# Weight tiles with 512 spare bytes, and blocks at changing offsets in them, in a float32 decoder layer

## The chip, the cores and the metric

The kernel runs on one core of one Trainium2 chip. The metric is device time in microseconds (us), from the start of the program to its end on that core.

## The reference

One layer of a hybrid decoder on 512 positions with 1024 channels, all in float32: half a gated FFN, a mixer, half a second gated FFN, a final norm.

```python
for l in range(DEPTH):                       # DEPTH = 1
    x = x + 0.5 * swiglu_ffn(rmsnorm(x, norm_ffn1[l]), ffn1_w_in[l], ffn1_w_out[l])
    x = x + hybrid_mixer(rmsnorm(x, norm_mix[l]), ...)
    x = x + 0.5 * swiglu_ffn(rmsnorm(x, norm_ffn2[l]), ffn2_w_in[l], ffn2_w_out[l])
return rmsnorm(x, norm_final)
```

`swiglu_ffn` is `(silu(x @ w_g) * (x @ w_u)) @ w_out` with 2816 hidden channels. The mixer projects to eleven parts of 1024 channels: a gated linear recurrence with 8 heads (HGRN2), a gated linear recurrence per channel (RG-LRU), a 31-tap causal convolution, and three gates. Each of the three branches is projected, gated and summed, and the sum goes through an output projection.

## The kernel before

**Numbers and products.** Each float32 operand is split into a high part (rounded to float32r, a form that TensorE multiplies faster) and a low part (the rest). A product is three matmuls: high weights with high activations (L255), high weights with low activations (L256), low weights with high activations (L257). A weight block is 128x128, the activations that stream past it are 128x512 (channels by positions).

**Weights.** All weights lie in DRAM in the order of use, in chunks of 16 blocks. `fetch` loads a chunk into one of two `raw` tiles. `_split_unit` (L214 to L239) turns half a chunk, a **unit** of 8 blocks, into a high tile `whi` (ScalarE, L230) and a low tile `wlo` (VectorE, L233). There are four buffers of each, and a unit is split two units before it is used. So a unit feeds 24 long matmuls. Units 0 to 43 are the first FFN's input weights, 44 to 65 its output weights, 66 to 185 the mixer's, 186 to 229 the second FFN's input weights, 230 to 251 its output weights. In all but the last stage the weights are the stationary operand, which TensorE loads ahead of a matmul. In the last stage (`last`, L533 to L535) four blocks side by side are a row of 512 columns that streams, and the activations are stationary.

**Pages.** Everything else of 128x512 lives in `NPAGES` pages of 2048 bytes per partition. `page` takes the oldest entry of the queue `free_pages`, `drop` puts a page at its end. A page's next owner waits until the last reader of the former one is done.

**Order.** The program is written in order of dependence, and a scheduler arranges the instructions of each engine by priorities that the kernel sets (`high_priority`, the filler taps of the convolution between other work, `issue_after`). On the chip each engine runs its list strictly in order.

**The mixer's parts that the prediction names.** `hgrn` (one call per head) makes `q` (L692) and `k`, then seven levels, each with small float32 matmuls on `q` and `k` (L749) and updates on VectorE; `dgs` and the state `st` end in the head's output (L776 with `dgs` as stationary operand, L778 with `q[:, t, :]`). `q` is a view of a tile with 132 columns per 128 positions:

```python
qx = self.tiny.tile([P, NTOK, P + 4], F32, tag="qx", name=self.name("q"), bufs=2)
q = qx[:, :, :P]
```

The 31-tap convolution is 30 VectorE operations per 128 channels (L607) that read and write `s` columns apart:

```python
s = CONVK - 1 - k
nc.vector.scalar_tensor_tensor(out=cv[1][:, s:], in0=cu[1][:, :S - s], scalar=w(k),
                               in1=cv[1][:, s:], op0=ALU.mult, op1=ALU.add)
```

`z` is the output of the second recurrence, eight pages, split at L297/L298 ahead of the projection of branch 1. `gw` are that recurrence's gate weights, four pages that are loaded and split (L297/L298) while the first FFN ends; they are first used at L632.

Of the kernel before, what the change touches and what calls it, by code (L numbers as in the profile page):

```python
# [12 lines left out]
F32R = mybir.dt.float32r  # L13
# [4 lines left out]
P = 128  # L18
# [112 lines left out]
    return m  # L131


class Kernel:
    NPAGES = 73
    CHUNK = 16
    UNIT = 8
    RBUFS = 2
# [10 lines left out]
    def __init__(self, ctx, tc, d):  # L149
# [5 lines left out]
        self.ps = ctx.enter_context(tc.tile_pool(name="ps", bufs=4, space=bass.MemoryType.PSUM))  # L155
        self.free_pages = deque(range(self.NPAGES))
        self.uid = 0
# [56 lines left out]
    def _split_unit(self):  # L214
        nc = self.nc
        u = self.next_unit
        if u * self.UNIT >= self.n_blocks:
            return
        per = self.CHUNK // self.UNIT
        c = u // per  # L220
        while self.next_raw <= c:
            self.fetch()
        o = (u % per) * self.UNIT
        raw = self.raws[c][:, o:o + self.UNIT, :]
        hi = self.ring.tile([P, self.UNIT, P], F32R, tag="whi", name=f"whi{u}", bufs=self.WBUFS)
        lo = self.ring.tile([P, self.UNIT, P], F32R, tag="wlo", name=f"wlo{u}", bufs=self.WBUFS)
        step = self.UNIT // 2 if u < 2 else self.UNIT
        for a in range(0, self.UNIT, step):
            z = slice(a, a + step)
            i = nc.scalar.activation(out=hi[:, z, :], in_=raw[:, z, :], func=AF.Copy)  # L230
            if u == self.MARK:
                self.mark = i
            self.last_lo = nc.vector.tensor_tensor(out=lo[:, z, :], in0=raw[:, z, :], in1=hi[:, z, :].bitcast(F32),  # L233
                                                   op=ALU.subtract)
        self.units[u] = (hi, lo)
        self.next_unit += 1
        if u % per == per - 1:
            del self.raws[c]
            self.fetch()  # L239
# [778 lines left out]
```

## Time and profile before

| | |
|---|---|
| Time, median of 3 runs | 1503.06 us (1501.24 to 1503.09) |
| Profiled execution: time | 1501.5 us |
| Profiled execution: span from first to last instruction | 1499.5 us |
| TensorE busy | 1486.5 us (99%), 6960 matmuls |
| VectorE busy | 897.3 us (60%) |
| ScalarE busy | 562.9 us (38%) |
| DMA, mean over the span | 93 GB/s, 139.55 MB |
| Granted TensorE clock, mean | 0.998 of full speed |

A row of the timeline has the start in us from the span's first instruction, the length in us, engine, line, operation and tiles as out<-in, with xN for N that follow each other, and in brackets the idle time before it with what ended it. Matmuls overlap: their starts tell the pace, and their lengths are longer than the step from one to the next. In a windows row, (xN) counts the instructions that reach into the window.

### The profile page before, as it was taken

Reading aid. Unit: us, or ns where it says so; the run is one execution under the profiler, and the core shown is the slowest. Engines: PE = TensorE matmul, PEld = TensorE weight load, DVE = VectorE, ACT = ScalarE, POOL = GpSimd, SP = SyncE. Lnnn points to the kernel's source line nnn. Section 1 sums busy time; section 2 is a strip of 40 time slices with the busy share of each in tenths; the row PEclk is TensorE's granted clock in tenths of the full one; section 3 lists DMA queues with packets and bytes.
Section 4 is the critical chain, followed back from the end, with each engine's and each line's share of the span. In section 5 each row is a group of like instructions: output and inputs, shape, how many; then the busy total and the mean of one; then the engine's idle time right before and its main releaser. Section 6 shows DMA issues by size and latency. Waiting matters only on the chain.

```text
span 1499.5 us, 17155 instructions
## 1 busy us (share of the span) xinstructions
PE 1486.5 (99%) x6960; PEld 1233.7 (82%) x6960; DVE 897.3 (60%) x1334; ACT 562.9 (38%) x822; POOL 21.8 (1%) x33
## 2 busy tenths in 40 slices
PE   9999999999999999999999999999999999999998
PEld 7888888888888888788887878888888888888887
DVE  7644444434877788898788995662554444444232
ACT  6322222223434345744456413453343222222122
POOL 0000000000000000000000000000000000000000
PEclk9999999999999999999999999999999999999999
DMA  6232322224222121212121222222232232322221
GB/s 239 85 113 85 102 95 90 107 85 141 84 90 108 57 85 60 82 61 81 57 85 56 85 97 101 84 98 99 87 110 85 84 112 85 101 97 102 109 85 56
DMA packets 22830, 139.55 MB, mean 93 GB/s; under 512 B 2656, under 2 KB 2912, under 8 KB 6880
## 3 DMA queue, kind: packets, MB, share of 16 engines
q1 hardware_dynamic: 22032, 137.41, 26.4%
q8 instruction: 55, 0.90, 0.2%
q10 hardware_dynamic: 720, 1.05, 0.2%
q14 instruction: 23, 0.19, 0.0%
HBM read 136.35 MB, written 2.10 MB: 92 GB/s over the span
## 4 chain that ended last, share of the span: by engine, by line
PE 66%; DVE 7%; ACT 2%; issue 1%; POOL 0%; POOLq 0%; ACTq 0%
PE acc L256 17%; PE acc L255 17%; PE acc L257 17%; DVE cv L607 3%; PE aux L749 3%; PE acc L534 2%; PE acc L535 2%; PE acc L533 2%; DVE wlo L233 1%; PE aux L533 1%; PE aux L534 1%; PE aux L535 1%; DVE th L670 1%; PE aux L739 0%; DVE gt L669 0%
## 5 line engine op out<-in xcount | busy, mean ns | idle before, releaser
L255 PE MATMUL acc<-hi,whi 128*128 128x512 f32 x1808 | 709.7, 393 | 0.2 <-ACT hi L305 0.2
L256 PE MATMUL acc<-lo,whi 128*128 128x512 f32 x1808 | 706.7, 391 | 1.0 <-DVE lo L298 1.0
L257 PE MATMUL acc<-hi,wlo 128*128 128x512 f32 x1808 | 706.9, 391 | 0.3 <-DVE wlo L233 0.3
L230 ACT ACTIVATE whi<-raw 128x1024 fp32r<-128x1024 f32 (+1 forms) x254 | 267.0, 1053 | 783.1 <-PE acc L256 526.1
L233 DVE TENSOR_TENSOR wlo<-raw,whi 128x1024 fp32r<-128x1024 f32 (+1 forms) x254 | 308.1, 1215 | 249.5 <-ACT whi L230 249.1
L257 PEld LDWEIGHTS acc<-hi,wlo 128*128 128x128 f32 x1808 | 339.8, 188 | 71.1 <-DVE wlo L233 0.7
L256 PEld LDWEIGHTS acc<-lo,whi 128*128 128x128 f32 x1808 | 340.0, 188 | 70.9 <-DVE lo L298 1.4
L255 PEld LDWEIGHTS acc<-hi,whi 128*128 128x128 f32 x1808 | 340.0, 188 | 70.2 <-issue 1.2
L607 DVE SCALAR_TENSOR_TENSOR cv<-cu,small,cv 128x507 f32<-128x507 f32 (+16 forms) x240 | 173.4, 732 | 3.3
L473 DVE TENSOR_TENSOR g<-g,acc 128x512 f32<-128x512 f32 x43 | 29.5, 687 | 107.6 <-PE acc L257 107.6
L470 DVE TENSOR_TENSOR g<-acc,bc 128x512 f32<-128x512 f32 x43 | 29.7, 691 | 101.8 <-PE acc L257 101.7
L749 PEld LDWEIGHTS aux<-q,k 128*127 128x127 f32 (+5 forms) x384 | 45.7, 183 | 11.1 <-DVE q L692 3.5
L749 PE MATMUL aux<-q,k 128*127 128x64 f32 (+5 forms) x384 | 46.5, 263 | 3.5 <-DVE q L692 3.0
L534 PE MATMUL acc<-wlo,hi 128*128 128x512 f32 (+1 forms) x132 | 46.7, 354 | 0.0
L535 PE MATMUL acc<-whi,lo 128*128 128x512 f32 (+1 forms) x132 | 46.7, 354 | 0.0
L533 PE MATMUL acc<-whi,hi 128*128 128x512 f32 (+1 forms) x132 | 46.6, 353 | 0.0
L752 DVE COPY_PREDICATED dgs<-masks,aux 127x256 f32<-127x256 uint8 (+4 forms) x40 | 26.5, 663 | 10.6 <-PE aux L749 10.3
L472 DVE TENSOR_TENSOR g<-g,sg 128x512 f32<-128x512 f32 x44 | 30.1, 686 | 0.7 <-ACT sg L471 0.7
L298 DVE TENSOR_TENSOR lo<-g,hi 128x512 fp32r<-128x512 f32 x44 | 30.0, 684 | 0.7 <-ACT hi L297 0.7
L297 ACT ACTIVATE hi<-g 128x512 fp32r<-128x512 f32 x44 | 27.0, 615 | 3.3 <-DVE g L473 3.3
L533 PEld LDWEIGHTS acc<-whi,hi 128*128 128x128 f32 x132 | 24.9, 189 | 4.1
L534 PEld LDWEIGHTS acc<-wlo,hi 128*128 128x128 f32 x132 | 24.9, 189 | 4.0
(204 smaller groups left out, 1010.0 us busy)
## 6 DMA issues: line engine op xcount, KB each, us to landing
raw<-w SPq DMA_DIRECT2D x124, 1024.0 KB, 4.8
x<-x SPq DMA_DIRECT2D x8, 256.0 KB, 6.0
raw<-w SPq DMA_DIRECT2D x8, 256.0 KB, 6.1
gw<-gw SPq DMA_DIRECT2D x4, 256.0 KB, 3.6
y<-xt SPq DMA_DIRECT2D x4, 256.0 KB, 2.1
y<-xt ACTq DMA_DIRECT2D x4, 256.0 KB, 2.5
gain<-nfin SPq DMA_DIRECT2D x2, 256.0 KB, 4.1
mk<-masks SPq DMA_DIRECT2D x1, 256.0 KB, 4.9
```

The costliest lines, as they stand in the source:

```text
L230: i = nc.scalar.activation(out=hi[:, z, :], in_=raw[:, z, :], func=AF.Copy)
L233: self.last_lo = nc.vector.tensor_tensor(out=lo[:, z, :], in0=raw[:, z, :], in1=hi[:, z, :].bitcast(F32), op=ALU.subtract)
L255: nc.tensor.matmul(out, lhsT=hi, rhs=xh[1], start=(k == 0), stop=False)
L256: nc.tensor.matmul(out, lhsT=hi, rhs=xl[1], start=False, stop=False)
L257: self.last_mm = nc.tensor.matmul(out, lhsT=lo, rhs=xh[1], start=False, stop=(k == n - 1))
L298: nc.vector.tensor_tensor(out=lo[1], in0=src, in1=hi[1].bitcast(F32), op=ALU.subtract)
L472: tt(out=g[1], in0=g[1], in1=sg[1], op=ALU.mult)
L533: nc.tensor.matmul(ps, lhsT=a, rhs=hi, start=(k == 0), stop=False)
L534: nc.tensor.matmul(ps, lhsT=a, rhs=lo, start=False, stop=False)
L535: nc.tensor.matmul(ps, lhsT=b, rhs=hi, start=False, stop=(k == FT - 1))
L607: nc.vector.scalar_tensor_tensor(out=cv[1][:, s:], in0=cu[1][:, :S - s], scalar=w(k), in1=cv[1][:, s:], op0=ALU.mult, op1=ALU.add)
L749: nc.tensor.matmul(pl[:w, t * 64:(t + 1) * 64].rearrange("p (b m) -> p b m", m=m), lhsT=k[1][:, t * P:t * P + w], rhs=ends(q[:, t, :], m), ...
```

## The change

Each `whi` and `wlo` tile is 128 float32 elements (512 bytes) longer. The 8 blocks of a unit lie together, but they begin at an element that `weight_offset` gives for the unit, for the high and the low tile apart. In the first FFN's input the offset starts at zero and grows by 64 bytes every five units, in its output only the low tile has one, in the second FFN's input it goes through 16, 32, 48, 96, 160, 224, 288, 352, 416, 480 and 8 bytes for four units each, in the second FFN's output by 64 bytes every three units. The mixer's units have none. The eight longer tiles take 4096 bytes per partition more; there is one page less.

```diff
--- before.py
+++ after.py
@@ -131,8 +131,24 @@
     return m
 
 
+def weight_offset(u):
+    if 4 <= u < 44:
+        a = 16 * ((u - 4) // 5)
+        return a, a
+    if 44 <= u < 65:
+        return 0, 16 * ((u - 44) // 3 + 1)
+    if 186 <= u < 230:
+        a = (4, 8, 12, 24, 40, 56, 72, 88, 104, 120, 2)[(u - 186) // 4]
+        return a, a
+    if 230 <= u < 251:
+        a = 16 * ((u - 230) // 3 + 1)
+        return a, a
+    return 0, 0
+
+
 class Kernel:
-    NPAGES = 73
+    NPAGES = 72
+    SLACK = 128
     CHUNK = 16
     UNIT = 8
     RBUFS = 2
@@ -222,8 +238,10 @@
             self.fetch()
         o = (u % per) * self.UNIT
         raw = self.raws[c][:, o:o + self.UNIT, :]
-        hi = self.ring.tile([P, self.UNIT, P], F32R, tag="whi", name=f"whi{u}", bufs=self.WBUFS)
-        lo = self.ring.tile([P, self.UNIT, P], F32R, tag="wlo", name=f"wlo{u}", bufs=self.WBUFS)
+        n = self.UNIT * P
+        wt = lambda what: self.ring.tile([P, n + self.SLACK], F32R, tag=what, name=f"{what}{u}", bufs=self.WBUFS)
+        hi, lo = [t[:, a:a + n].rearrange("p (b n) -> p b n", n=P)
+                  for t, a in zip((wt("whi"), wt("wlo")), weight_offset(u))]
         step = self.UNIT // 2 if u < 2 else self.UNIT
         for a in range(0, self.UNIT, step):
             z = slice(a, a + step)
```

The offsets alone leave every engine's list as it was. With one page less the queue of free pages turns sooner, and the scheduler arranges some places differently. Three of them follow. (The diff adds 18 lines, so that L255 to L257 read L273 to L275 after it, L230 reads L248, L297 L315, L305 L323, L316 L334, L702 L720, L749 L767, L910 L928.)

**Before the mixer**, ScalarE, where the first FFN ends. `gw258` to `gw267` are the four tiles of gate weights, `x9` is the last of the eight `x` tiles, `hi211` its high part. Before:

```order
L230 ACTIVATE whi68_2532<-raw34_2426 128x1024
L297 ACTIVATE hi259_2740<-gw258_2738 128x512
L230 ACTIVATE whi69_2570<-raw34_2426 128x1024
L297 ACTIVATE hi262_2746<-gw261_2744 128x512
L297 ACTIVATE hi265_2752<-gw264_2750 128x512
L297 ACTIVATE hi268_2758<-gw267_2756 128x512
L305 ACTIVATE hi211_2524<-x9_97,small_70 128x512
L316 ACTIVATE sq213_2528<-x9_97 128x512
```

After the change:

```order
L248 ACTIVATE whi68_2532<-raw34_2426 128x1024
L248 ACTIVATE whi69_2570<-raw34_2426 128x1024
L315 ACTIVATE hi259_2740<-gw258_2738 128x512
L315 ACTIVATE hi262_2746<-gw261_2744 128x512
L323 ACTIVATE hi211_2524<-x9_97,small_70 128x512
L334 ACTIVATE sq213_2528<-x9_97 128x512
L315 ACTIVATE hi265_2752<-gw264_2750 128x512
L315 ACTIVATE hi268_2758<-gw267_2756 128x512
```

The split and the square of `x9` have moved ahead of the last two `gw` splits, and one weight tile ahead of the first.

**Head 7**, TensorE, at its start. `vf636` are the values that are transposed, `q633` and `k635` the head's first level, `acc658` the first gate projection that fills in between. Before:

```order
L257 MATMUL acc632_5978<-hi249_2659,wlo129_5906 128x512
L702 MATMUL aux638_6024<-ident_71,vf636_6021 128x128 x4
L255 MATMUL acc658_6135<-hi228_2617,whi130_5947 128x512
L256 MATMUL acc658_6135<-lo229_2618,whi130_5947 128x512
L257 MATMUL acc658_6135<-hi228_2617,wlo130_5948 128x512
L749 MATMUL aux642_6036<-q633_6012,k635_6016 127x64 x4
L255 MATMUL acc658_6135<-hi231_2623,whi130_5947 128x512
```

After the change:

```order
L275 MATMUL acc632_5978<-hi249_2659,wlo129_5906 128x512
L273 MATMUL acc658_6135<-hi228_2617,whi130_5947 128x512
L274 MATMUL acc658_6135<-lo229_2618,whi130_5947 128x512
L720 MATMUL aux638_6024<-ident_71,vf636_6021 128x128 x4
L275 MATMUL acc658_6135<-hi228_2617,wlo130_5948 128x512
L273 MATMUL acc658_6135<-hi231_2623,whi130_5947 128x512
L274 MATMUL acc658_6135<-lo232_2624,whi130_5947 128x512
L275 MATMUL acc658_6135<-hi231_2623,wlo130_5948 128x512
L273 MATMUL acc658_6135<-hi234_2629,whi130_5947 128x512
L767 MATMUL aux642_6036<-q633_6012,k635_6016 127x64 x4
```

Two matmuls of `acc658` have moved ahead of the transposes, and two more stand between these and the first level.

**The start of branch 1**, TensorE. `hi690` and `lo691` are the high and low part of the last `z`, `acc692` to `acc694` the first three outputs. Before, `hi690` is used at once in all three, and the wait is for `lo691`:

```order
L255 MATMUL acc694_6541<-hi678_6441,whi140_6470 128x512
L256 MATMUL acc694_6541<-lo679_6442,whi140_6470 128x512
L257 MATMUL acc694_6541<-hi678_6441,wlo140_6471 128x512
L255 MATMUL acc694_6541<-hi680_6445,whi140_6470 128x512
L256 MATMUL acc694_6541<-lo681_6446,whi140_6470 128x512
L256 MATMUL acc692_6469<-lo691_6466,whi138_6365 128x512
L257 MATMUL acc692_6469<-hi690_6465,wlo138_6366 128x512
```

After the change:

```order
L275 MATMUL acc694_6541<-hi682_6449,wlo140_6471 128x512
L273 MATMUL acc694_6541<-hi684_6453,whi140_6470 128x512
L274 MATMUL acc694_6541<-lo685_6454,whi140_6470 128x512
L275 MATMUL acc694_6541<-hi684_6453,wlo140_6471 128x512
L273 MATMUL acc692_6469<-hi690_6465,whi138_6365 128x512
L273 MATMUL acc693_6504<-hi690_6465,whi139_6401 128x512
L273 MATMUL acc694_6541<-hi686_6457,whi140_6470 128x512
L274 MATMUL acc692_6469<-lo691_6466,whi138_6365 128x512
L275 MATMUL acc692_6469<-hi690_6465,wlo138_6366 128x512
```

The matmuls with `hi690` and `lo691` now stand together, behind more of `acc694`.

In the same stretch ScalarE's row of `hi690` has moved. `sg` are gate values. Before:

```order
L230 ACTIVATE whi137_6327<-raw68_6176 128x1024
L910 ACTIVATE sg665_6280<-acc664_6244,small_70 128x512
L297 ACTIVATE hi690_6465<-z617_5825 128x512
L230 ACTIVATE whi138_6365<-raw69_6249 128x1024
L910 ACTIVATE sg669_6324<-acc668_6290,small_70 128x512
L230 ACTIVATE whi139_6401<-raw69_6249 128x1024
```

After the change:

```order
L928 ACTIVATE sg673_6398<-acc672_6364,small_70 128x512
L248 ACTIVATE whi141_6505<-raw70_6331 128x1024
L928 ACTIVATE sg675_6435<-acc674_6400,small_70 128x512
L315 ACTIVATE hi690_6465<-z617_5825 128x512
L248 ACTIVATE whi142_6542<-raw71_6405 128x1024
L248 ACTIVATE whi143_6577<-raw71_6405 128x1024
```

The row stands behind four more pairs of weight tile and gate. The page that it writes was `cu293` until then, which VectorE's last tap of the convolution reads.

## Rows read from the trace of the kernel before

**Rows 1.** The page's first lines: span, then busy time of TensorE and its loads.
```profile
span 1499.5 us, 17155 instructions
PE 1486.5 (99%) x6960; PEld 1233.7 (82%) x6960; DVE 897.3 (60%) x1334; ACT 562.9 (38%) x822; POOL 21.8 (1%) x33
```

**Rows 2.** Windows view, all engines, a stretch of the first FFN.
```profile
core 0: us, PE busy (x) PEld busy (x) DVE busy (x) ACT busy (x) POOL busy (x), PEclk, DMA share, GB/s
60.00:360.00 300.00, 300.00 (x1325) 248.47 (x1325) 131.05 (x153) 84.79 (x104) 0.00 (x0) 1.00 0.28 95
```

**Rows 3.** Timeline of TensorE in the last stage, 128x256 matmuls: start, length, what.
```profile
1487.11 0.28 PE L533 MATMUL acc<-whi,hi 128*128 128x256 f32 x1
...
1487.83 0.28 PE L533 MATMUL acc<-whi,hi 128*128 128x256 f32 x1
```

**Rows 4.** The page's costliest groups, the two that write the weight tiles.
```profile
L230 ACT ACTIVATE whi<-raw 128x1024 fp32r<-128x1024 f32 (+1 forms) x254 | 267.0, 1053 | 783.1 <-PE acc L256 526.1
L233 DVE TENSOR_TENSOR wlo<-raw,whi 128x1024 fp32r<-128x1024 f32 (+1 forms) x254 | 308.1, 1215 | 249.5 <-ACT whi L230 249.1
```

**Rows 5.** Timeline of TensorE in a mixer head, the output of head 2.
```profile
604.23 0.38 PE L778 MATMUL aux<-st,q 128*128 128x128 f32 x2
604.45 0.39 PE L776 MATMUL aux<-v,dgs 128*128 128x128 f32 x2
604.60 0.48 PE L257 MATMUL acc<-hi,wlo 128*128 128x512 f32 x1
...
605.14 0.38 PE L778 MATMUL aux<-st,q 128*128 128x128 f32 x2
605.28 0.47 PE L256 MATMUL acc<-lo,whi 128*128 128x512 f32 x1
```

**Rows 6.** Groups by shape: two of VectorE's 30 tap sizes.
```profile
L607 DVE SCALAR_TENSOR_TENSOR cv<-cu,small,cv 128x508 f32<-128x508 f32 x8 | 6.0, 744 | 0.1
L607 DVE SCALAR_TENSOR_TENSOR cv<-cu,small,cv 128x507 f32<-128x507 f32 x8 | 6.0, 744 | 0.1
```

**Rows 7.** Timeline before the mixer: ScalarE, then TensorE.
```profile
370.56 0.63 ACT L297 ACTIVATE hi<-gw 128x512 fp32r<-128x512 f32 x1 [0.80 <-DMA gw<-gw]
371.10 0.71 ACT L305 ACTIVATE hi<-x,small 128x512 fp32r<-128x512 f32 x1
...
371.25 0.39 PE L257 MATMUL acc<-hi,wlo 128*128 128x512 f32 x1
371.86 0.74 PE L255 MATMUL acc<-hi,whi 128*128 128x512 f32 x2 [0.22 <-ACT hi L305]
...
373.34 1.02 PE L335 MATMUL aux<-ones,sq 128*128 128x1 f32 x8
...
374.55 0.40 PE L255 MATMUL acc<-hi,whi 128*128 128x512 f32 x1
```

**Rows 8.** Timeline of TensorE at the start of head 7.
```profile
804.47 0.50 PE L257 MATMUL acc<-hi,wlo 128*128 128x512 f32 x1 [0.26 <-DVE wlo L233]
...
806.26 1.50 PE L749 MATMUL aux<-q,k 128*127 128x64 f32 x8 [1.30 <-DVE q L692]
```

**Rows 9.** Windows view behind that place; PEclk is the granted clock.
```profile
806.80:810.20 3.40, 3.40 (x12) 2.85 (x11) 2.73 (x8) 0.84 (x2) 0.00 (x0) 0.50 0.71 280
```

**Rows 10.** Timeline at the start of branch 1: VectorE and TensorE.
```profile
863.66 9.11 DVE L607 SCALAR_TENSOR_TENSOR cv<-cu,small,cv 128x488 f32<-128x488 f32 x14
...
872.03 0.39 PE L256 MATMUL acc<-lo,whi 128*128 128x512 f32 x1
...
872.69 0.68 DVE L298 TENSOR_TENSOR lo<-z,hi 128x512 fp32r<-128x512 f32 x1
...
873.43 0.50 PE L256 MATMUL acc<-lo,whi 128*128 128x512 f32 x1 [1.01 <-DVE lo L298]
```

**Rows 11.** Timeline of TensorE in a head with the other order, head 5.
```profile
737.48 0.49 PE L778 MATMUL aux<-st,q 128*128 128x128 f32 x2
737.80 0.39 PE L776 MATMUL aux<-v,dgs 128*128 128x128 f32 x2
```

## The prediction

> **What bounds the kernel now.** The page first [rows 1]: TensorE is busy 1486.5 of 1499.5 us. The reader is to see that nothing else comes near, so a change counts only where it alters the step from one matmul to the next, or TensorE's few waits. Then a window of the first FFN without a wait [rows 2]: 1325 matmuls in 300 us at a granted clock of 1.00. A matmul is counted while its 0.39 us last, so the step is (300 + 0.39) / 1325 = 226.7 ns. Each has its weight load beside it (248.47 us for 1325, 187.5 ns): the load is 39 ns shorter than the step and is not the bound. In the last stage 256 columns step by 0.72 us / 6 = 120 ns [rows 3], so 256 columns more cost 106.7 ns, 512 cost 213.3, and **a fixed 13.3 ns** is left in every matmul. That part is what an address might touch.
>
> **What the offsets move.** By the table, units 4 to 8, 65, 66 to 185 and 251 stay at zero. With an offset: units 9 to 43 (both tiles, 35 x 24 = 840 matmuls), 44 to 64 (the low tile alone, 21 x 8 = 168), 186 to 229 (both, 44 x 24 = 1056) and 230 to 250, where the weights stream (11 x 24 in the first half, 10 x 30 in the second, 564). Together 2628. Buffers lie 4608 instead of 4096 bytes apart, so every address also shifts by multiples of 512 bytes; in [rows 2] eight blocks, four buffers and some seventy pages already meet in all such combinations at one step.
>
> Offsets inside 512 bytes are new for these matmuls, so no row prices them directly. Bounds: the fixed part vanishes, or comes a second time, 13.3 ns x 2628 = 35.0 us either way. The nearest row says zero. In the mixer `q[:, t, :]` is a stationary operand with 528 bytes between blocks, so blocks at 16, 32 and 48 bytes past a 512-byte step from the tile's start, while `dgs` lies on the step. Just before a long matmul two passes on `dgs` take 604.60 - 604.45 = 0.15 us, two on `q` 605.28 - 605.14 = 0.14 [rows 5]. These are 128-column matmuls of plain float32, hence a hint and no proof. I take **0**.
>
> A rule against any gain: the Trainium skill (TensorE: Matmul & The Clock Gate, Step-by-step: what each phase is for) gives the engine separate read ports for streaming operand and weights, so a load takes no bandwidth from the running matmul. By that rule offsets can't unlock the 13.3 ns, and the sum is the same as by the row. The same page states 215.7 ns for a warm 512-column step; the trace's 226.7 is 11 ns over it, for float32r with a new load each time, and if an offset brought the page's value, 2628 x 11 = 29 us would go. No row here shows such a step.
>
> The tiles are written by ScalarE (1053 ns per high tile) and VectorE (1215 per low) [rows 4]. A unit lasts 24 x 226.7 = 5.44 us on TensorE and tiles are made two units ahead, so even a doubled write stays under it; without that cover 254 x 1.2 us = 309 us would show. The taps write at 4-byte steps: 508 columns (16 bytes in) and 507 (20 bytes in) both 744 ns [rows 6]. So zero here too.
>
> **What one page less moves.** The eight tiles take 4096 bytes, a page is 2048; with 72 pages the queue of free pages turns one step earlier, waits for pages change, and the scheduler orders three places differently (the order rows above). Nothing else in the order depends on the offsets.
>
> *Before the mixer.* ScalarE's split of the last `x` stands behind four splits of `gw`, of which the last waits for its transfer; it starts at 371.10 and TensorE waits for it, then for VectorE's low part [rows 7]. From 371.25 to 374.55 pass 3.30 us for seven long matmuls (1.59) and the eight column sums (1.21 - 0.23 = 0.98): 0.73 lost, of which entering the sums keeps about 0.13. Now only two `gw` splits stand ahead, and VectorE updates `x` before the 1.2 us low tile, not after it. The split starts about 2 us earlier. **-0.6 us** (0 to -0.7). The delayed `gw` splits are needed only by the gate matmuls (L632), deep in the mixer.
>
> *Head 7.* One long matmul starts at 804.47, and the first level, which waits for VectorE's `q`, at 806.26 [rows 8]: 1.79 - 0.23 = 1.56 us lost. Now four long matmuls more stand ahead of the level, so 0.9 of it is filled. Right behind it the granted clock is 0.50 from 806.8 to 810.2 [rows 9], which costs up to 1.7 us and followed this gap; a shorter gap may keep it away.
>
> *Start of branch 1.* VectorE's taps run without a gap to 872.69, then the low part of the last `z`; TensorE stands from 872.03 + 0.23 to 873.43, 1.17 us [rows 10]. This is VectorE's time: what TensorE gains in head 7 it waits out here. VectorE's list has as many operations ahead of this one as before. But the high part, once made long before, now waits for a page which the last tap frees: it comes 0.63 us after the taps, the low part another 0.68 later, with ScalarE's next weight tile queued behind it (that one waits for the same matmuls, and TensorE is two units ahead of it). Against it TensorE has five more long matmuls (1.13 us) before it needs the high part and three between high and low. High part at 872.69 + 0.68, TensorE ready at 872.26 + 1.13 = 873.39: the wait is gone where VectorE and TensorE keep their times. So head 7 and branch 1 together give 1.13 us with VectorE unmoved, up to 2.0 if it too gets through head 7 sooner. **-1.1 us**.
>
> *Head 6.* Two matmuls on `st` come sooner behind the copy that they need. In heads with this order the pair takes 0.32 instead of 0.22 us [rows 5, 11]: **+0.1 us**, to +0.7 if the table load nearby falls badly.
>
> Sum: 0 - 0.6 - 1.1 + 0.1 = **-1.6 us**. The profiled execution took 1501.5 us (1499.5 of span) and would take 1499.9. Its time is the lower end of the three before (1501.24 to 1503.09); against their median of 1503.06 the sum gives 1501.4, 0.1% less, where about 0.2% (3 us) is what a measurement of this kernel can tell from no change.
>
> **Rivals.**
> 1. *Offsets slow the reads.* A block at a new offset costs the fixed part again. If only offsets that are no multiple of 64 bytes do it, units 186 to 229 pay 1056 x 13.3 = 14 us: 1515. If all do, 35 us: 1536. It decides from 3 / 2628 us, 1.1 ns per matmul. For it: the fixed part exists, and nothing in the trace streams float32r from such an address. Against: [rows 5, 6]. The Trainium skill (SBUF — State Buffer, Specifications (TRN2)) has 16-byte lines with a penalty for each one entered; by it only the 8-byte offset, units 226 to 229, reads a line more, 96 matmuls, and the tally stays under 1.3 us even at the full 13.3 ns. No run here shows that.
> 2. *Offsets part weights from the streamed rows.* The fixed part is a collision of both reads, which lie on the same 512-byte step in every long matmul, and goes at some offsets: at half of them -17 us, 1484; at all -35, 1466. For it: 13.3 ns that no wait explains. Against: both walk through all low addresses in each matmul anyway, and `q` is no faster than 0.01 us over two passes.
> 3. *The order gains more.* The clock drop of [rows 9] goes and VectorE gets through head 7 a microsecond sooner: -1.6 - 1.7 - 0.9 = -4.2, 1498.9. Against: branch 1 waits for VectorE, which takes most of what TensorE wins ahead of it.
> 4. *The order loses.* The split chain behind the last tap (0.63 + 0.68) isn't covered and the idle brings another stretch at half clock, +1.7: about +2 to +3.5, 1505 to 1506.5.
> That the change doesn't do what it says is hardly open: the blocks do lie at the offsets, and zero effect is the forecast itself.
>
> **How the numbers follow.** Offsets without effect and the order within 3 us: 64%, alone 1499.5 to 1504. Rival 1: 14% (a third of it within 7 us). Rival 2: 4%. Rival 3: 13%. Rival 4: 5%, mostly under 3 us. The time is that of the first: 1501.4. The range leaves out rival 2, the strongest of rival 3 and the upper two thirds of rival 1: 1498.3 to 1508. Faster by over 0.2%: rival 2 and most of 3, 16%. Slower: rival 1, some of 4, and a tail of the first, 18%. Same: 66%.
>
> **What would show it.** Right: matmuls at 226.7 ns in every window of units 9 to 64 and 186 to 251, with no step at the changes of offset (every five, three or four units); the high tile still at 1053 ns; no wait for the split of `x` before the mixer; a shorter gap in head 7; the high part of the last `z` made behind the last tap. Wrong: a staircase in the matmul steps of the first or last FFN, a low-tile-only change between units 44 and 64, or a wait on `whi` or `wlo`.

## Result

The changed kernel takes 1515.71 us in the median (1513.39 to 1515.76), 1.0083 times the kernel before (95% interval 1.0060 to 1.0106), so 12.5 us slower (9 to 16). The prediction was 1501.4 us, with a range up to 1508.0: wrong, and on the wrong side. What came true is rival 1, in a form between its two cases.

The page of the changed kernel, its span and its busy engines, answers to [rows 1]:

```profile
span 1513.7 us, 17146 instructions
PE 1500.2 (99%) x6960; PEld 1234.3 (82%) x6960; DVE 897.8 (59%) x1334; ACT 559.8 (37%) x820; POOL 22.2 (1%) x33
```

TensorE has the same 6960 matmuls and is busy 13.7 us longer; VectorE's time is within 0.5 us of what it was, and ScalarE's is shorter. So it is the pace of the matmuls, or the same idle time counted elsewhere; the windows view decides which. Each window here runs from the first matmul of a group of units to the first of the next, so that it holds a known number of matmuls; the weight loads (PEld) count them, give or take one at an edge:

```profile
57.10:85.10 28.00, 28.00 (x122) 22.56 (x120) 12.59 (x15) 7.90 (x10) 0.00 (x0) 1.00 0.26 91
85.10:112.99 27.89, 27.89 (x122) 22.61 (x121) 12.58 (x15) 7.91 (x10) 0.00 (x0) 1.00 0.29 100
112.99:140.46 27.47, 27.47 (x121) 22.54 (x120) 12.58 (x15) 7.91 (x10) 0.00 (x0) 1.00 0.25 91
140.46:167.68 27.22, 27.22 (x121) 22.53 (x120) 12.58 (x15) 7.90 (x10) 0.00 (x0) 1.00 0.30 100
167.68:195.67 27.99, 27.99 (x121) 22.57 (x120) 12.59 (x15) 7.90 (x10) 0.00 (x0) 1.00 0.26 92
251.04:267.68 16.64, 16.64 (x74) 13.52 (x72) 6.12 (x7) 3.68 (x4) 0.00 (x0) 1.00 0.31 106
300.98:317.30 16.32, 16.32 (x74) 13.52 (x73) 6.50 (x8) 4.43 (x5) 0.00 (x0) 1.00 0.25 91
1384.87:1401.36 16.49, 16.49 (x73) 13.52 (x72) 4.96 (x5) 3.68 (x4) 0.00 (x0) 1.00 0.34 114
1418.10:1434.90 16.80, 16.80 (x74) 13.54 (x72) 3.68 (x3) 3.19 (x3) 0.00 (x0) 1.00 0.31 101
```

This is the staircase that the prediction named as the sign of its failure. The first five windows are units 9 to 13 (64 bytes), 14 to 18 (128), 19 to 23 (192), 24 to 28 (256) and 29 to 33 (320), 120 matmuls each: 28.00 / 120 = 233.3 ns, then 232.4, 228.9, at 256 bytes 226.8, the old step of [rows 2] but for the 0.02 us at the change of group, and at 320 bytes 233.3 again. Units 34 to 43 (384 and 448 bytes) go on with 232.5 and 228.9: **the period is 256 bytes**. The next two windows are units 44 to 46 and 53 to 55, 72 matmuls each, with the low tile alone at 64 and 256 bytes: 231.1 and 226.7 ns. In the last two the weights stream: 64 bytes give 229.0, 192 give 233.3, the other way round than in the first group. The granted clock is 1.00 in all nine, and TensorE is busy throughout: no wait, no throttle, each matmul simply starts later.

The split of the weights kept its pace, as said: 1054 and 1214 ns against the 1053 and 1215 of [rows 4]. From the page's costliest groups:

```profile
L248 ACT ACTIVATE whi<-raw 128x1024 fp32r<-128x1024 f32 (+1 forms) x254 | 267.2, 1054 | 796.8 <-PE acc L274 519.3
L251 DVE TENSOR_TENSOR wlo<-raw,whi 128x1024 fp32r<-128x1024 f32 (+1 forms) x254 | 308.0, 1214 | 250.1 <-ACT whi L248 249.6
```

Of the three places where the order moved, the timeline of the changed kernel shows, in this order, TensorE before the mixer, TensorE in head 7, and VectorE, ScalarE and TensorE at the start of branch 1 (the answers to [rows 7, 8, 10]):

```profile
377.88 0.39 PE L275 MATMUL acc<-hi,wlo 128*128 128x512 f32 x1
378.11 0.94 PE L353 MATMUL aux<-ones,sq 128*128 128x1 f32 x8
...
812.58 0.50 PE L275 MATMUL acc<-hi,wlo 128*128 128x512 f32 x1 [1.28 <-DVE wlo L251]
...
814.38 0.88 PE L767 MATMUL aux<-q,k 128*127 128x64 f32 x6 [0.35 <-DVE q L710]
...
871.42 8.45 DVE L625 SCALAR_TENSOR_TENSOR cv<-cu,small,cv 128x488 f32<-128x488 f32 x13
...
879.90 0.63 ACT L315 ACTIVATE hi<-z 128x512 fp32r<-128x512 f32 x1 [11.96 <-DVE cv L625]
...
880.58 0.96 PE L273 MATMUL acc<-hi,whi 128*128 128x512 f32 x3 [1.23 <-ACT hi L315]
```

Before the mixer the wait for the split is gone. In head 7 the wait for `q` shrank from 1.30 to 0.35 us, but a wait of 1.28 for the low weight tile stands ahead of it. At branch 1 the high part is made behind the last tap, as said, and TensorE waits 1.23 us for it.

### The profile page after: what moved, and what is told of

It reads as the page before. It is cut to its first block, busy times and chain, and to the rows that moved or that the text cites. A ratio compares the mean times of both kernels' runs of the same rounds, so it can differ in the third digit from the quotient of the medians.

```text
span 1513.7 us, 17146 instructions
## 1 busy us (share of the span) xinstructions
PE 1500.2 (99%) x6960; PEld 1234.3 (82%) x6960; DVE 897.8 (59%) x1334; ACT 559.8 (37%) x820; POOL 22.2 (1%) x33
## 4 chain that ended last, share of the span: by engine, by line
PE 91%; DVE 6%; ACT 1%; issue 1%; DMA 0%; POOL 0%; SPq 0%; POOLq 0%; ACTq 0%
PE acc L273 25%; PE acc L274 25%; PE acc L275 25%; DVE cv L625 3%; PE aux L767 3%; PE acc L551 2%; PE acc L553 2%; PE acc L552 2%; DVE wlo L251 1%; PE aux L552 1%; PE aux L553 1%; PE aux L551 1%; DVE th L688 1%; PE aux L757 0%; DMA raw<-w 0%
## 5 line engine op out<-in xcount | busy, mean ns | idle before, releaser
L273 PE MATMUL acc<-hi,whi 128*128 128x512 f32 x1808 | 713.2, 395 | 1.2 <-ACT hi L315 1.2
L275 PE MATMUL acc<-hi,wlo 128*128 128x512 f32 x1808 | 711.6, 394 | 1.3 <-DVE wlo L251 1.3
L248 ACT ACTIVATE whi<-raw 128x1024 fp32r<-128x1024 f32 (+1 forms) x254 | 267.2, 1054 | 796.8 <-PE acc L274 519.3
L251 DVE TENSOR_TENSOR wlo<-raw,whi 128x1024 fp32r<-128x1024 f32 (+1 forms) x254 | 308.0, 1214 | 250.1 <-ACT whi L248 249.6
L273 PEld LDWEIGHTS acc<-hi,whi 128*128 128x128 f32 x1808 | 340.3, 188 | 75.2 <-ACT hi L315 1.7
L275 PEld LDWEIGHTS acc<-hi,wlo 128*128 128x128 f32 x1808 | 340.2, 188 | 75.3 <-DVE wlo L251 1.5
L625 DVE SCALAR_TENSOR_TENSOR cv<-cu,small,cv 128x507 f32<-128x507 f32 (+21 forms) x240 | 173.4, 732 | 3.3
L767 PEld LDWEIGHTS aux<-q,k 128*127 128x127 f32 (+5 forms) x384 | 45.3, 182 | 10.6 <-DVE q L710 2.7
L767 PE MATMUL aux<-q,k 128*127 128x64 f32 (+5 forms) x384 | 46.2, 262 | 2.7 <-DVE q L710 2.0
L316 DVE TENSOR_TENSOR lo<-g,hi 128x512 fp32r<-128x512 f32 x44 | 30.0, 684 | 0.7 <-ACT hi L315 0.7
L315 ACT ACTIVATE hi<-g 128x512 fp32r<-128x512 f32 x44 | 27.0, 616 | 3.2 <-DVE g L491 3.2
```

The lines of the kernel that those rows point to most:

```text
L273: nc.tensor.matmul(out, lhsT=hi, rhs=xh[1], start=(k == 0), stop=False)
L275: self.last_mm = nc.tensor.matmul(out, lhsT=lo, rhs=xh[1], start=False, stop=(k == n - 1))
L316: nc.vector.tensor_tensor(out=lo[1], in0=src, in1=hi[1].bitcast(F32), op=ALU.subtract)
L767: nc.tensor.matmul(pl[:w, t * 64:(t + 1) * 64].rearrange("p (b m) -> p b m", m=m), lhsT=k[1][:, t * P:t * P + w], rhs=ends(q[:, t, :], m), ...
```

## Experiments

**Theory 1**: the step of a float32r matmul depends on the address of its stationary block relative to its streamed rows, modulo 256 bytes. **Theory 2**: each operand has preferred addresses of its own, and the costs add. **Theory 3**: page count and order cost the time, and the offsets only coincide with it. Ratios below are to the kernel before, run beside each.

**Order and longer tiles alone** (slack0), against the changed kernel:

```diff
 def weight_offset(u):
-    if 4 <= u < 44:
...
     return 0, 0
```

> The longer tiles and the 72 pages stay, every offset is zero: the new order and the 4608-byte spacing alone. Theory 1 (the step of a long matmul depends on the address of its weights relative to its streamed rows, modulo 256 bytes) and theory 2 (each operand has preferred addresses of its own): steps back at 226.7 ns in units 9 to 64 and 186 to 251, and 1500 to 1503.5 us, the order's -1.6 us being about all that is left. Theory 3 (the pages and the order cost the time, the offsets only coincide with it): 1513 to 1516 us.

1500.67 us, ratio 0.9992 (0.9983 to 1.0000). The windows of units 9 to 13, 44 to 46 and 230 to 232:

```profile
57.15:84.35 27.20, 27.20 (x122) 22.52 (x120) 12.59 (x15) 7.90 (x10) 0.00 (x0) 1.00 0.26 94
247.55:263.87 16.32, 16.32 (x74) 13.51 (x72) 6.10 (x7) 3.67 (x4) 0.00 (x0) 1.00 0.32 102
1371.04:1387.36 16.32, 16.32 (x73) 13.51 (x72) 4.96 (x5) 3.67 (x4) 0.00 (x0) 1.00 0.35 113
```

226.7 ns in all three. Theory 3 falls, and the prediction's term for the order (-1.6 us) lies inside the interval of -2.6 to 0.

**Offsets with the old order** (offsets73), against the changed kernel:

```diff
-    NPAGES = 72
+    NPAGES = 73
```

> The offsets with 73 pages, so with the instruction order of the kernel before. From the steps in the trace of the changed kernel the offsets cost about 3.5 us in units 9 to 43, 1.9 in 44 to 64, 6.9 in 186 to 229 and 1.5 to 2 in 230 to 250, together 14. Theories 1 and 2: the same staircase, 1515 to 1518 us. Theory 3: 1501 to 1504 us.

1514.40 us, ratio 1.0085 (1.0071 to 1.0099). The offsets alone are the loss.

**Weights and pages moved together** (shift_all), against the kernel before, at the head of its constants:

```diff
+        self.const.tile([P, 16], F32, name="shift")
```

> The kernel before with 64 bytes more in front of its buffers: weight tiles and pages all move by 64 bytes and keep their addresses relative to each other. Theory 1: nothing changes, 1501 to 1504 us and 226.7 ns. Theory 2: every long matmul pays what 64 bytes on both tiles cost in units 9 to 13, 6.7 ns, over some 6,000 of them 40 us: about 1543 us. Theory 3: no change, since the order is that of before.

1502.94 us, ratio 1.0008 (0.9999 to 1.0018); units 9 to 13 as before:

```profile
56.92:84.12 27.20, 27.20 (x122) 22.52 (x120) 12.59 (x15) 7.90 (x10) 0.00 (x0) 1.00 0.26 94
```

Both operands lie 64 bytes further and nothing happens. Theory 2 falls for steps of 64 bytes, and with it the story that 64 bytes are bad by themselves; finer common steps are another matter (map1 below).

**Weights and pages moved apart** (pad192, pad64): the kernel before, with a tile of 48 or 16 words ahead of the pages.

```diff
         self.pgs = ctx.enter_context(tc.tile_pool(name="pgs", bufs=1))
+        self.pgs.tile([P, 48], F32, name="pad")
```

> The kernel before with 192 bytes between the weight tiles and the pages, so that every weight block lies 64 bytes past its rows modulo 256; no offset, 73 pages, the old order. Theory 1 (relative address modulo 256): 5520 matmuls with stationary weights at 6.67 ns more, 36.8 us, and in the last stage, where the weights stream and the relation is turned round (192), 264 x 2.2 ns and as much again for its half-width part: together about 38 us, 1539 to 1543 us where the kernel before takes 1502 or 1503. Theory 3 (pages and order) and a theory in which an offset inside a tile costs by itself: no change.

> The same with 64 bytes between weight tiles and pages: weights at 192 past their rows, in the last stage at 64. Theory 1: 5520 x 2.23 ns = 12.3 us, and 264 x 6.67 = 1.8 us and about 1 us more in the last stage: 1516 to 1519 us, and steps of 228.9 ns in the first feed-forward and 233.3 in the first half of the last stage, the reverse of the run with 192. A theory in which the size of the pad counts and not its place modulo 256 would give the 64 bytes a third of what 192 give.

With 192 bytes 1531.85 us, ratio 1.0201 (1.0184 to 1.0218); with 64 bytes 1513.00, ratio 1.0075 (1.0059 to 1.0090). Units 9 to 13 and 230 to 232, first with 192 bytes:

```profile
58.42:86.42 28.00, 28.00 (x122) 22.44 (x120) 12.60 (x15) 7.91 (x10) 0.00 (x0) 1.00 0.25 88
1401.33:1418.13 16.80, 16.80 (x74) 13.61 (x72) 4.97 (x5) 3.72 (x4) 0.00 (x0) 1.00 0.30 99
```

then with 64:

```profile
56.85:84.32 27.47, 27.47 (x121) 22.54 (x120) 12.59 (x15) 7.91 (x10) 0.00 (x0) 1.00 0.26 91
1381.87:1398.67 16.80, 16.80 (x74) 13.47 (x73) 4.97 (x5) 3.71 (x4) 0.00 (x0) 1.00 0.29 97
```

In the feed-forward both are as computed, 233.3 and 228.9 ns: a pad of 16 unused words costs the tuned kernel 11 us, one of 48 words 30 us. Two misses. First, the sums of 38 and 14 to 16 us came out as 30 and 11. From unit 9 to 65 the 192 bytes cost 313.60 - 304.64 = 8.96 us, exactly 1344 x 6.67 ns, but from unit 65 to 186, where the long matmuls stand among short ones and TensorE waits for other engines, 11.7 instead of 19.4. Part of that is known: the kernel before pays there already (402 of its 2783 steps last 228 to 245 ns), and its profiled execution loses 1.5 us to half clock there ([rows 9], worked out below), which this one doesn't. Second, the last stage with 192 bytes steps by 233.3, where Theory 1 said 228.9. It keeps 233.3 up to unit 241, where the first half-width matmuls come, and goes on at 228.9 behind them.

**Offsets of 256 bytes only** (off256), against the changed kernel, in each of its four groups:

```diff
-        a = 16 * ((u - 4) // 5)
+        a = 64 * ((u - 4) // 5 % 2)
```

> The changed kernel with every other group of units at 256 bytes and the rest at zero. Theory 1: no cost, as with all offsets at zero, 1499.5 to 1503 us, 226.7 ns everywhere. If an offset costs by being inside the tile or by leaving a 512-byte step, half the units pay: 6 to 9 us more.

1500.40 us, ratio 0.9989 (0.9980 to 0.9999). Units 9 to 13, here at 256 bytes:

```profile
56.90:84.10 27.20, 27.20 (x121) 22.52 (x120) 12.59 (x15) 7.93 (x10) 0.00 (x0) 1.00 0.26 95
```

It is 226.7 ns there and in the other groups. An offset costs nothing as such. The 0.1% against the kernel before is level with slack0, which has the same order and no offset.

**The matmuls alone, over a table of addresses** (map1): stationary blocks at s bytes and streamed rows at m past a common base, in a kernel of nothing else.

```python
CELLS = [(s, m) for m in (0, 16, 32, 48) for s in range(0, 64, 4)]   # 4-byte words
...
for i, (l, r) in enumerate(((hi, xh), (hi, xl), (lo, xh))):
    nc.tensor.matmul(acc, lhsT=l, rhs=r, ...)
```

> Matmuls 128x512 of float32r alone, 48 in each of 76 cells, in the order high-high, high-low, low-high: the weights lie at s bytes from a 256-byte step relative to the streamed rows' base (16-byte steps to 240), the streamed rows at 0, 64, 128 or 192; then 4 and 8 bytes on either side. The reference's computation is left out. Theory 1: cells with s = m all at 226.7 ns whatever m; s - m = 64 at 233.3, 128 at 232.3, 192 at 228.9, so that the four rows of the table are one row turned by 64 bytes each. Theory 2: one row adds a constant to another, and 64 on both sides costs at least 6.7 ns. If neither, cells where s - m is equal differ and cells don't add up either. No cell is expected below 226.7 ns; one at 221 or less would show that the fixed part of the step can be saved.

The timeline has one row for each cell; a, e, i and m stand for 0, 64, 128 and 192 bytes, b and f for 16 and 80, of the weights (w) and the rows (x):

```profile
21.71 11.05 PE L170 MATMUL wb_xa<-x,w 128*128 128x512 f32 x48
...
54.98 11.36 PE L170 MATMUL we_xa<-x,w 128*128 128x512 f32 x48
99.74 11.37 PE L170 MATMUL wi_xa<-x,w 128*128 128x512 f32 x48
144.37 11.15 PE L170 MATMUL wm_xa<-x,w 128*128 128x512 f32 x48
188.65 11.17 PE L170 MATMUL wa_xe<-x,w 128*128 128x512 f32 x48
232.96 11.04 PE L170 MATMUL we_xe<-x,w 128*128 128x512 f32 x48
...
677.97 11.04 PE L170 MATMUL wm_xm<-x,w 128*128 128x512 f32 x48
...
722.12 11.20 PE L170 MATMUL wb_xb<-x,w 128*128 128x512 f32 x48
...
755.13 11.36 PE L170 MATMUL wf_xf<-x,w 128*128 128x512 f32 x48
```

A cell lasts 47 steps and a last matmul of 0.39 us: (11.04 - 0.39) / 47 = 226.6 ns where both lie alike at 64, 128 or 192 bytes, 233.4 for 64 bytes apart, 233.6 for 128, 228.9 for 192, and 229.4 for rows 64 past the weights, which is 192 the other way round. The four rows of the table are one row, turned by 64 bytes each. The one blemish is 128 bytes apart: by the starts of the matmuls 233.3 in three of the four cells and 232.3 in the fourth, against 232.4 in the kernel. No cell of the table is below 226.6: the kernel before already lies at the best address, since its weight tiles and pages are all multiples of 512 bytes long.

The last cells limit Theory 1. Weights 16 bytes past rows at 0 still take 226.8 ns. But with weights and rows both at 16 bytes the step is 230.0 ns (231.1 in map2), both at 80 bytes 233.4, and both at 48 bytes 230.0, although they lie alike. In the map2 run below, rows at 32 bytes follow the table (226.7 ns with the weights at 32, 233.3 with them at 0 or 64), while rows at 16 bytes have their best at weights 32 bytes further (226.8 ns) and their worst at 16 further (236.6). So the relative address decides where the rows start at a multiple of 32 bytes (0, 32, 64, 128 and 192 were tried), and the kernels' steps follow that table but for the relations with two paces under Open; at 8, 16, 48 and 80 bytes the place of the rows counts as well, and neither theory gives the step.

**Fewer columns, other types** (map2), the same kernel with other shapes:

> Matmuls alone again, 48 per cell; the reference's computation is left out. Weights at 0, 64, 128, 192 bytes past the rows' 256-byte step, with 64 and 32 stationary columns instead of 128, with 384 and 256 streamed columns, with 64 rows instead of 128; plain float32 with 128 and 512 streamed columns; bfloat16 at 32-byte steps; and weights at 16-byte steps beside rows at 16 and 32 bytes. Theory 1a (the weight load and the running stream contend for as long as both read): the extra time shrinks with the stationary columns, at 64 bytes 6.7 ns with 128, about 3.3 with 64, 1.7 with 32, and the fixed 13.3 ns shrinks too, to 6.7 and 3.3, a step of 220 and 217 ns. Theory 1b (only the start of a load is put off, once for each matmul): 6.7 ns and 226.7 ns with any number of columns. For 64 rows both expect what 128 rows show if all partitions read alike. For plain float32 with 128 columns the row that the prediction leaned on says no cost at 16 to 48 bytes; open at 64 and 128.

Rows of the timeline, in their order: 64 stationary columns at 0 bytes, 32 at 0, 256 streamed columns at 0 and at 64; bfloat16 at 0 and 128; plain float32 with 128 streamed columns at 0 and 128, with 512 at 0 and 64 (two instructions for each matmul); float32r weights at 32 beside rows at 16:

```profile
21.98 11.20 PE L184 MATMUL m_b<-x_r,w_r 128*64 128x512 f32 x48
33.02 11.29 PE L184 MATMUL m_c<-x_r,w_r 128*32 128x512 f32 x48
...
52.49 5.91 PE L184 MATMUL n_e<-x_r,w_r 128*128 128x256 f32 x48
...
111.31 5.61 PE L184 MATMUL n_c<-x_r,w_r 128*128 128x256 f32 x48
...
245.65 10.53 PE L184 MATMUL b_a<-x_b,w_b 128*128 128x512 bf16 x48
...
287.10 10.52 PE L184 MATMUL b_e<-x_b,w_b 128*128 128x512 bf16 x48
...
328.54 10.88 PE L184 MATMUL f_a<-x_f,w_f 128*128 128x128 f32 x96
...
392.86 10.88 PE L184 MATMUL f_g<-x_f,w_f 128*128 128x128 f32 x96
...
414.30 41.37 PE L184 MATMUL g_a<-x_f,w_f 128*128 128x512 f32 x96
455.50 41.36 PE L184 MATMUL g_b<-x_f,w_f 128*128 128x512 f32 x96
...
518.91 11.51 PE L184 MATMUL s_e<-x_r,w_r 128*128 128x512 f32 x48
```

Both Theories 1a and 1b fall. With half or a quarter of the stationary columns the step at 0 bytes does not shrink, nor stay: it grows, (11.20 - 0.39) / 47 = 230.0 and 231.9 ns. With 256 streamed columns the sign turns: 64 bytes are faster, (5.61 - 5.91) / 47 = 6.4 ns less. So it is no cost per byte read together. One part of 1a does hold: the spread over 0, 64, 128 and 192 bytes shrinks with the stationary columns, from 6.6 ns with 128 to 4.1 with 64 (228.4 to 232.5) and 1.1 with 32, by the starts. Half the rows (64 instead of 128) change nothing; 384 streamed columns take 173.3 ns at 0, 64 and 192 bytes and 175.8 at 128. Of the three types only float32r shows a dependence. All eight bfloat16 cells (32-byte steps) last alike, 215.8 ns, and so do all eight of plain float32 with 128 columns, 0 to 192 bytes.

**Memory and single operands** (map3), 96 matmuls per cell:

> Matmuls alone, 96 per cell; the reference's computation is left out. First a walk through weights at 0, 64, 128 and 192 bytes past the rows in which each follows each other once; then one of the four operands alone displaced (high tile, low tile, high rows, low rows) by 64, 128 and 192; then one pair of operands only, three times the same. Theory 1 as it stands: 226.7, 233.3, 232.3 and 228.9 ns whatever came before. If the step has a memory (both operands stay in the relation in which they were caught), 192 after 64 stays at 233.3, as in the last stage of the run with 192 bytes, and is 228.9 only after others. Displaced alone: if the relation of each pair counts by itself, the low tile at 64 gives 231.1 as in units 44 to 64, the high tile more (two of three pairs), the low rows about what the low tile gives.

Timeline rows in their order: 64, 128 and 192 bytes, each after 0; 64 after 192, 192 after 64, 192 after 128; then the high tile alone at 64, the low tile, the high rows, the low rows:

```profile
32.75 22.56 PE L171 MATMUL c_b<-x,w 128*128 128x512 f32 x96
...
76.95 22.48 PE L171 MATMUL c_d<-x,w 128*128 128x512 f32 x96
...
121.05 22.14 PE L171 MATMUL c_f<-x,w 128*128 128x512 f32 x96
143.03 22.56 PE L171 MATMUL c_g<-x,w 128*128 128x512 f32 x96
...
210.13 22.14 PE L171 MATMUL c_j<-x,w 128*128 128x512 f32 x96
...
254.41 22.15 PE L171 MATMUL c_l<-x,w 128*128 128x512 f32 x96
...
298.17 22.56 PE L171 MATMUL c_n<-x,w 128*128 128x512 f32 x96
320.57 22.35 PE L171 MATMUL c_o<-x,w 128*128 128x512 f32 x96
342.75 22.54 PE L171 MATMUL c_p<-x,w 128*128 128x512 f32 x96
365.13 22.43 PE L171 MATMUL c_q<-x,w 128*128 128x512 f32 x96
```

By (length - 0.39) / 95 the step is 233.4 at 64 and 228.9 to 229.1 at 192 whatever relation came before: no memory of it, and so the 233.3 of the last stage with 192 bytes isn't explained by it. One displaced operand of four is enough: 233.4, 231.2, 233.2 and 232.0. The low tile gives the 231.1 of units 44 to 46. One pair of operands repeated, in place of the three products, has the steps of the walk: 226.8, 233.4, 232.5 and 229.0.

## Why the prediction was wrong

**The step that failed** is in "What the offsets move": "Offsets inside 512 bytes are new for these matmuls, so no row prices them directly", and then "I take **0**", from "the nearest row". The offsets cost 13.6 us: by the starts of the same units in the changed kernel and in the one with zero offsets, (251.04 - 57.10) - (247.55 - 57.15) = 3.5 us in units 9 to 43, 1.95 in 44 to 64, 6.7 in 186 to 229 and 1.4 in the last stage. Over 2628 matmuls that is 5.2 ns each, inside the bounds of 13.3 either way and far over the 1.1 from which rival 1 decides. The fixed 13.3 ns behind those bounds is no constant: by the same sum the relation of 64 bytes gives 2 x 113.3 - 233.3 = -6.7 ns (map2).

**The row was right and didn't apply.** `q` and `dgs` of [rows 5] do step alike; the plain float32 cells show the same at every offset tried. But plain float32 streams 512 columns in 429.2 ns for each of two instructions, where float32r takes 226.7 for one. The note "a hint and no proof" was in the text; the chance of 64% for no effect didn't follow it. Nor could [rows 2] help: its buffers meet in all multiples of 512 bytes, and the cost has a period of 256.

**The rule against a gain** misled too. By the Trainium skill (TensorE: Matmul & The Clock Gate, Step-by-step: what each phase is for) a load takes no bandwidth from the running matmul. The bfloat16 cells agree, and their 215.8 ns is within 0.1 of the warm step that the page states; for float32r the address of the weights against the rows moves the step by 6.7 ns in the changed kernel, so there the two are not independent. The rule of 16-byte lines in the Trainium skill (SBUF — State Buffer, Specifications (TRN2)), as the prediction read it, would have put a cost on the 8-byte offset alone. The trace of the changed kernel has the larger cost at whole lines: by the starts of 96 matmuls each 230.7 ns at 8 bytes, 233.3 at 32 and 233.2 at 48. At 16 bytes it has 233.2 in unit 189, where map1 has 226.7.

**Rival 1** had the sign and a price per matmul of up to 13.3 ns, of which 6.7 came; its split was wrong: multiples of 64 bytes are no safe class, multiples of 256 are. That its first case, 1515 us, lies beside the measured 1515.7 is luck: it charged 13.3 ns to 1056 matmuls, where 5.2 ns fell on each of 2628. Rival 2, "a collision of both reads, on the same 512-byte step", had the pair that counts and the sign reversed: on the same step they are at their best.

**The writes** stayed: 1054 ns for the high tile and 1214 for the low, against 1053 and 1215.

**The order's -1.6 us** was measured as -1.2 (-2.6 to 0). The sum of its parts did not come true. *Before the mixer*, said -0.6: from unit 65 to the first of the matmuls on `dg` 361.79 to 379.06 with the new order, 361.28 to 379.36 before, -0.8. From there to a matmul at 703.6 us, ahead of the last three heads, it takes 324.5 against 324.3, a loss of 0.2 that the prediction had no place for. *Head 6*, *head 7* and *branch 1*, together -1.0: from that matmul to the same one behind branch 1's start (949.64 before) it is 246.0 us before and 245.1 with zero offsets, which looks right. But the profiled execution of before has the half clock of [rows 9] in it. Two others in the old order, without it there and with no offset in this stretch (offsets73, shift_all), take 244.4 and 244.5; the three in the new order 245.1, 245.2 and 245.1. So the half clock took 1.5 us, and the order itself loses 0.6: in all -0.8 + 0.2 + 0.6 = 0. The wait for the low tile in head 7 took the place of that for `q`, and branch 1 waits for VectorE, as rival 3's counterargument said. The stretch does not belong to that one gap: the changed kernel has such a stretch too, in the head before, with 0.51 granted:

```profile
631.90:635.30 3.40, 3.40 (x11) 2.72 (x10) 3.40 (x7) 0.00 (x0) 0.00 (x0) 0.51 0.67 272
```

and four of the eight executions profiled (before, changed, shift_all, pad64) have one, the other four none, with either order. How often it comes is what differs. With a mean granted clock of 0.999 the kernel before spans 1498.0 to 1498.6 us, and the new order with offsets that cost nothing (slack0, off256) 1497.9 to 1498.8, so at an equal clock the order is worth nothing (no execution profiled at 0.999 has such a stretch); but 6 of 34 runs of the kernel before have that clock, none of the 10 of shift_all, and 17 of the 21 in the new order. So the measured -1.2 us is the first half of rival 3, fewer stretches at half clock, and not the waits that the sum counted. Why the new order has fewer is not shown.

**Open** stays what in the chip sets the step. Two pairs of steady steps lie 6.67 ns apart (226.7 and 233.3; 113.3 and 120.0 for 256 columns), which is 16 periods of 2.4 GHz; others lie between (228.9, 230.0, 231.1). Some relations have two steady paces (128 bytes: 232.4 and 233.3; 192 in the last stage with the pad: 233.3 and 228.9; 16 bytes in offsets73: 233.3 in unit 187, and 226.7 in unit 188, behind two other matmuls). A stream and a load that fall into step with each other would look so; nothing here shows it.

## What to carry over

Where float32r matmuls with 512 streamed columns run back to back, start the streamed rows at a multiple of 64 bytes and the stationary blocks at the same address modulo 256 bytes: a pad of 16 words between them cost 11 us here, and no wait in the profile shows it. Look for it in the step between the starts of equal matmuls, or in the length of a window with a known number of them. The price taken from the nearest row held here only for its own data type and pace of stream; where those differ, the bounds deserve the weight, or one micro-kernel.

## Unexpected of the hardware

- A float32r matmul of 128x512 steps by 226.7 to 236.6 ns by its operands' addresses alone (236.6 with weights at 32 and rows at 16 bytes); bfloat16 takes 215.8 at all eight offsets.
- Moving weights and rows together by 64 bytes costs nothing; both at 16 bytes step by 230.0 ns, both at 80 by 233.4.
- 256 columns take 120.0 ns with weights and rows on the same step and 113.3 with 64 bytes between them.
- Fewer stationary columns make a float32r matmul longer: 226.7 ns with 128, 230.0 with 64, 231.9 with 32.
